# Block sums of the second MLP weights: adding transfers in place of VectorE sums

## The chip, the cores and the metric

The kernel runs on one core of one Trainium2 chip. The metric is the device time of one execution in microseconds. Most executions of a kernel agree within 0.3%. A profile is taken of one further execution by the hardware profiler; its span runs from the first instruction to the last. The engines are TensorE (PE in the profile; its weight loads are the row PEld), VectorE (DVE), ScalarE (ACT), GpSimd (POOL) and SyncE (SP). SP and GpSimd issue the DMAs of this kernel; SP's transfers and GpSimd's run through different DMA queues.

## What is computed

Two decoder layers over 512 tokens of width 1024, in fp32. Each layer has a token mixer (a state-space mixer in layer 0, a gated linear recurrence in layer 1), a normalization, an MLP with 4096 hidden units, another normalization, and a gated input embedding. The change touches the MLP alone:

```python
def sq_relu_mlp(h, w1, w2):
    a = jax.nn.relu(h @ w1)
    return (a * a) @ w2

# in each layer i
h = layer_norm(DEEPNORM_ALPHA * x + mix, ln_g[i, 0], ln_b[i, 0])
h = layer_norm(DEEPNORM_ALPHA * h + sq_relu_mlp(h, mlp_w1[i], mlp_w2[i]), ln_g[i, 1], ln_b[i, 1])
x = h + jax.nn.sigmoid(h @ ple_w_gate[i]) * (p[i] @ ple_w_proj[i])
```

## The kernel before

**Precision.** Every fp32 product is made of three matmuls (`mm3`, lines 119-122): each operand is split into a high and a low part, and high x high, high x low and low x high are added up in PSUM. `split` (lines 109-117) makes the two parts of a weight tile of 128x1024: ScalarE casts it into `whi` (line 113), VectorE subtracts that from the tile and writes `wlo` (line 116). Each of `whi` and `wlo` has six buffers. `unit` (lines 102-107) loads a weight tile through SP into one of three `raw` buffers and splits it.

**The MLP** (`mlp_and_gate`, lines 558-670). The hidden units fall into four groups of 1024. A tile of the first weights, T, is one `project`: 24 matmuls of 128x512 give 128 hidden units for all tokens; ReLU and square follow on ScalarE. Eight tiles make a group. Each group's product with the second weights is a 2x2 block product with seven multiplications in place of eight (the Strassen-Winograd scheme): the hidden activations are cut into blocks a11, a12, a21, a22, the weights into blocks w[0][0], w[0][1], w[1][0], w[1][1], and sums of blocks are multiplied. `half_blocks` (lines 300-320) makes the sums of activations on VectorE and splits each with `put`; it runs twice in a group, once for each half of its tiles. `weight_sums` (lines 322-345) makes the four sums of weight blocks, t1 to t4.

**The weight sums before.** In `weight_sums`, GpSimd issues eight plain loads of 512 KB (line 329) for one group: two halves of each of the four blocks, into eight tiles tagged `r`. VectorE then makes eight sums in place (lines 336, 339, 340 and 344, each for two halves). The tag `r` has eight buffers, all used by one group, so the loads of the next group wait until the splits of this one have read theirs. The same function serves the value projection between the two layers (`values4`, line 675), where the change leaves it as it is.

**The products** (`block_product`, lines 347-395). A product Q is two PSUM banks (c = 0, 1), each of 12 matmuls. `product` splits its weights, multiplies, and lets VectorE empty each bank into the accumulator `acc` (lines 373, 377 and 379); in the last group it also makes row sums for the normalization (line 373). Three sums of products share PSUM: "x" (two banks of the pool `psy`, named `py0` and `py1`) gathers four products one after the other, being read out after each; "y" gathers two and "z" has one (pool `psj`). The products are called p1 (a11), p2 (a12), p3 (s4), p4 (a22), p5 (s1), p6 (s2), p7 (s3), by the activation block that they use.

**The order.** `PERIODS` (line 32) sets how tiles and products alternate: eight T for the first group; then three times two T and seven Q with a T between each two, so that the products of a group run among the tiles of the next; and seven Q without any T for the last group. Inside such a period the products came as p1, p2, p6, p7, p5, p4, p3, and in the last group as p1, p7, p6, p4, p5, p2, p3. Each engine works through its own list in order. A scheduler makes these lists when the kernel is built, from priorities and modelled costs; `high_priority(offset=...)` moves instructions ahead, by `LEAD` = 100, `SOON` = 40 or the group's entry of `SUMS` (line 33). In the MLPs TensorE's order is the scheduler's as well, so that the matmuls of neighbouring products can mix.

**Behind the last group**: the second normalization (`norm`), transposes, and the gate. In the second MLP that is `last_gate` (lines 397-556), which uses four more `r` tiles and already makes its own weight sums with transfers that add onto what is in SBUF (lines 401-408, `accum_op=ALU.add`), issued by GpSimd.

Of the kernel before, what the change touches and what calls it, by code (L numbers as in the profile page):

```python
# [12 lines left out]
ALU = mybir.AluOpType  # L13
PSUM = bass.MemoryType.PSUM

P = 128
# [7 lines left out]
ALPHA = 4.0 ** 0.25  # L24
EPS = 1e-5
LEAD = 100
# [6 lines left out]
SUMS = (60, 300, 300, 300)  # L33
# [11 lines left out]
def trunk(ctx: ExitStack, tc, a):  # L45
    nc = tc.nc
# [21 lines left out]
    def mk(p, shape, tag, dt=F32, **kw):  # L68
        return p.tile(list(shape), dt, tag=tag, name=nm(tag), **kw)

    def f32(t):
        return t.bitcast(F32)
# [16 lines left out]
    def tmp(tag, shape, dt=F32):  # L89
        return mk(phase[0], shape, tag, dt, bufs=phase[2].get(tag, 1))  # L90

    def bank(p, tag):
        return mk(p, [P, T], tag)
# [8 lines left out]
    def unit(src, lead=LEAD, after=None):  # L102
        n = src.shape[1]
        with tc.high_priority(offset=lead):
            raw = mk(raws, [P, 1024], "raw")
            nc.sync.dma_start(raw[:, :n], src)
        return split(raw[:, :n], lead, after)

    def split(f, lead=LEAD, after=None):
        n = f.shape[1]  # L110
        with tc.high_priority(offset=lead):
            hi = mk(whip, [P, 1024], "whi", F32R)
            nc.scalar.copy(hi[:, :n], f)  # L113
            lo = mk(wlop, [P, 1024], "wlo", F32R)
            with behind(after):
                nc.vector.tensor_sub(lo[:, :n], f, f32(hi[:, :n]))  # L116
        return hi, lo

    def mm3(out, sh, sl, mh, ml, start, stop, **kw):
        nc.tensor.matmul(out, sh, mh, start=start, stop=False, **kw)  # L120
        nc.tensor.matmul(out, sh, ml, start=False, stop=False, **kw)  # L121
        return nc.tensor.matmul(out, sl, mh, start=False, stop=stop, **kw)  # L122
# [26 lines left out]
    with tc.high_priority(offset=FIRST):  # L149
        zero = nc.const_aps.tensor(0.0, (P, 1), F32)  # L150
        ps = bank(psm, "pm")
# [76 lines left out]
    def behind(ins):  # L228
        return tc.issue_after(ins.ins) if ins is not None else nullcontext()
# [70 lines left out]
    def half_blocks(blk, z0, z1, p):  # L300

        ks = slice(2 * p, 2 * p + 2)
        a11, a12, a21, a22 = z0[:, :, 256:], z1[:, :, 256:], z0[:, :, :256], z1[:, :, :256]

        def put(name, f):
            hi, lo = blk[name][:, 0, ks, :], blk[name][:, 1, ks, :]
            nc.scalar.copy(hi, f)
            nc.vector.tensor_sub(lo, f, f32(hi))

        put("a11", a11)  # L310
        put("a22", a22)
        nc.vector.tensor_add(a22, a21, a22)
        put("a12", a12)
        nc.vector.tensor_sub(a21, a11, a21)
        nc.vector.tensor_sub(a11, a22, a11)
        nc.vector.tensor_sub(a12, a12, a11)
        put("s2", a11)
        put("s3", a21)
        put("s1", a22)
        put("s4", a12)  # L320

    def weight_sums(w, lead, after=None, queue=nc.gpsimd):

        t = [None] * 4
        for i in (2, 1, 3, 0):
            t[i] = [tmp("r", [P, 1024]) for _ in range(2)]

        def load(i, u, src):
            queue.dma_start(t[i][u], src)  # L329

        with tc.high_priority(offset=lead):
            for u in range(2):
                load(0, u, w[0][1][u])
                load(2, u, w[1][1][u])
                with behind(after):
                    nc.vector.tensor_sub(t[2][u], t[2][u], t[0][u])
                load(1, u, w[0][0][u])
                with behind(after):
                    nc.vector.tensor_sub(t[0][u], t[0][u], t[1][u])
                    nc.vector.tensor_add(t[1][u], t[2][u], t[1][u])  # L340
            for u in range(2):
                load(3, u, w[1][0][u])
                with behind(after):
                    nc.vector.tensor_sub(t[3][u], t[3][u], t[1][u])
        return t

    def block_product(w, blk, lead, first, after=None, turns=None, sums=None, low=None):

        t1, t2, t3, t4 = weight_sums(w, lead, after=low)
        seen = set() if first else {(i, j) for i in range(2) for j in range(2)}
        banks = {}

        def product(x, f, name, start, i, j, turns=None):
            us = [split(v) if f in (t1, t2, t3, t4) else unit(v) for v in f]
            if start:
                banks[name] = [bank(psy, "py%d" % c) if name == "x" else bank(psj, "pj") for c in range(2)]
            t = blk[x]
            for c in range(2):  # L360
                ps = banks[name][c]
                sl = slice(c * P, (c + 1) * P)
                for k in range(4):
                    hi, lo = us[k // 2]
                    ks = slice((k % 2) * 512, (k % 2 + 1) * 512)
                    w_ = hi[:, ks], lo[:, ks]
                    mm3(ps, t[:, 0, k, sl], t[:, 1, k, sl], *w_, start and k == 0, k == 3, skip_group_check=True)
                    if turns and (c, k) in ((0, 3), (1, 1)):
                        next(turns)
                d = acc[:, 2 - 2 * i + c, j * 512 : (j + 1) * 512]  # L370
                with tc.high_priority(offset=SOON if after else 0):
                    if after and f in (w[1][0], t1, t4, w[1][1]):
                        nc.vector.tensor_tensor_reduce(
                            d, ps, d, 1.0, 0.0, ALU.add, ALU.add, sums[:, 2 - 2 * i + c, j : j + 1]
                        )
                    elif (i, j) in seen:
                        nc.vector.tensor_add(d, ps, d)
                    else:
                        nc.vector.scalar_tensor_tensor(d, d, ALPHA, ps, ALU.mult, ALU.add)
            seen.add((i, j))  # L380

        p1 = lambda: product("a11", w[0][0], "x", True, 0, 0)
        p2 = lambda: product("a12", w[1][0], "z", True, 0, 0)
        p6 = lambda: product("s2", t2, "x", False, 1, 0)
        p7 = lambda: product("s3", t3, "y", True, 1, 1)
        p5 = lambda: product("s1", t1, "x", False, 1, 1)
        p4 = lambda: product("a22", t4, "y", False, 1, 0)
        p3 = lambda: product("s4", w[1][1], "x", False, 0, 1, turns)
        for f in (p1, p7, p6, p4, p5, p2, p3) if after else (p1, p2, p6, p7, p5, p4, p3):
            f()  # L390
            if after and f is p5:
                after(0), after(1)
            if after and f is p3:
                after(2), after(3)
            yield
# [162 lines left out]
    def mlp_and_gate(layer, h_s, last):  # L558

        w1, w2 = a[f"w1_{layer}"], a[f"w2_{layer}"]  # L560
        blocks = {}
        low = turned_last[0]
# [32 lines left out]
        for g, period in enumerate(PERIODS):  # L595
            if g < 4:
                tiles = hidden(g)
            if g > 0:
                if g == 4:
                    kept = tmp("blk", [P, 2, 4, 256]) if last else None  # L600
                    h_s, after, turned, sums = norm(2 * layer + 1, kept)
                    p_s = (mk(w4, [P, 2, T], "a", F32R), mk(w4, [P, 2, T], "b", F32R))
                    praw = mk(raws, [P, 1024], "raw")
                    nc.sync.dma_start(praw, a[f"pT_{layer}"].rearrange("p k t -> p (k t)"))
                    praw = praw.rearrange("p (k t) -> p k t", k=2)
                    nc.scalar.copy(p_s[0], praw)
                    nc.vector.tensor_sub(p_s[1], praw, f32(p_s[0]))
                w = [[[w2[8 * g - 8 + 4 * i + 2 * j + u] for u in range(2)] for j in range(2)] for i in range(2)]
                products = block_product(w, blocks.pop(g - 1), SUMS[g - 1], g == 1, *((after, turned(0), sums) if g == 4 else ()), low=low if g == 1 else None)
            for op in period:  # L610
                next(tiles if op == "T" else products)

# [29 lines left out]
        for h in range(2):  # L642
            pu = unit(a[f"wp_{layer}"][h])
            gu = [unit(a[f"wg_{layer}"][4 * h + j]) for j in range(4)]
            for c in range(NCH):
                sl = slice(c * P, (c + 1) * P)
                if h == c == 0:
                    turns = turned(1)
# [6 lines left out]
                turns = turned(c + 2) if h == 0 and c < 2 else None  # L655
# [9 lines left out]
                d = acc[:, c, h * 512 : (h + 1) * 512]  # L665
# [66 lines left out]
    ps = bank(psj, "pj")  # L732
    first = [bank(psy, "py0"), bank(psy, "py1"), bank(psj, "pj"), bank(psj, "pj")]
    for k in range(8):
        if k == 4:
            for i in range(8):
                for c in range(NCH):
# [4 lines left out]
                        start=i == 0,  # L742
# [227 lines left out]
    for j in range(17):  # L970
# [6 lines left out]
        if pend is not None:  # L977
            i = j - 1
# [4 lines left out]
            y = tmp("y", [P, T])  # L983
# [3 lines left out]
            for _, n, done, y in half if i % 2 or i >= 14 else ():  # L987
                done()
                w = snw[:, n : n + 1]
# [13 lines left out]
    g, s, ss = outs.pop(0)  # L1003
# [460 lines left out]
```

## Time and profile before

| | us |
|---|---|
| median of 3 runs | 1411.94 |
| lowest and highest of them | 1411.82, 1413.4 |
| span of the profiled execution | 1409.6 |
| TensorE matmul busy | 1404.3 |
| weight loads busy | 1168.1 |
| VectorE busy | 1069.1 |
| ScalarE busy | 763.6 |
| GpSimd busy | 45.8 |

The span is 2.3 us below the median; that much lies around the first and the last instruction. The granted TensorE clock is 1.000 over the whole span. DMAs moved 181.69 MB, 41.95 MB of them through GpSimd's queue.

How to read the rows that follow. A group's row names line, engine and operation, then output tile and input tiles by their names, the shape, the count, then busy time in us and the mean of one in ns, and after the second bar the idle time of that engine just before, with what ended most of it. A timeline's row begins with the start and the duration in us. A row of waits reads: who waited, for whom, in total, how many times, and the longest. Matmuls overlap on TensorE, so a matmul's duration is longer than the distance between the starts of two.

### The profile page before, as it was taken

Reading aid. Unit: us, or ns where it says so; the run is one execution under the profiler, and the core shown is the slowest. Engines: PE = TensorE matmul, PEld = TensorE weight load, DVE = VectorE, ACT = ScalarE, POOL = GpSimd, SP = SyncE. Lnnn points to the kernel's source line nnn. Section 1 sums busy time; section 2 is a strip of 40 time slices with the busy share of each in tenths; the row PEclk is TensorE's granted clock in tenths of the full one; section 3 lists DMA queues with packets and bytes.
Section 4 is the critical chain, followed back from the end, with each engine's and each line's share of the span. In section 5 each row is a group of like instructions: output and inputs, shape, how many; then the busy total and the mean of one; then the engine's idle time right before and its main releaser. Section 6 shows DMA issues by size and latency. Waiting matters only on the chain.

```text
span 1409.6 us, 20400 instructions
## 1 busy us (share of the span) xinstructions
PE 1404.3 (100%) x8001; PEld 1168.1 (83%) x8001; DVE 1069.1 (76%) x1778; ACT 763.6 (54%) x1156; POOL 45.8 (3%) x92
## 2 busy tenths in 40 slices
PE   9999999999999999999999999999999999999998
PEld 7888888888988888888888888888898888888887
DVE  7989688698977668677986577678785867667795
ACT  7766465573354444545555547655555454544573
POOL 0000000001000000000000000000100000000100
PEclk9999999999999999999999999999999999999999
DMA  8433333234433444345621421222443444444731
GB/s 313 135 117 120 106 120 110 85 100 156 141 113 127 157 131 152 129 142 178 209 90 49 134 91 61 76 87 96 150 135 105 147 137 148 144 137 159 202 106 60
DMA packets 50399, 181.69 MB, mean 129 GB/s; under 512 B 5632, under 2 KB 6400, under 8 KB 50176
## 3 DMA queue, kind: packets, MB, share of 16 engines
q1 hardware_dynamic: 38784, 138.45, 29.6%
q0 software_dynamic: 11520, 41.95, 9.2%
q8 instruction: 63, 1.03, 0.3%
q14 instruction: 32, 0.26, 0.1%
HBM read 177.16 MB, written 2.16 MB: 127 GB/s over the span
## 4 chain that ended last, share of the span: by engine, by line
PE 99%; DMA 0%; DVE 0%; issue 0%; DVEq 0%
PE pj L120 25%; PE pj L121 25%; PE pj L122 25%; PE py L120 5%; PE py L122 5%; PE py L121 5%; PE py L906 1%; PE pt L238 1%; PE py L1175 1%; PE pm L923 1%; PE pm L871 1%; PE py L1301 1%; PE pt L859 0%; PE py L1303 0%; PE py L1240 0%; PE py L832 0%
## 5 line engine op out<-in xcount | busy, mean ns | idle before, releaser
L113 ACT CAST whi<-raw 128x1024 fp32r<-128x1024 f32 x218 | 228.8, 1050 | 333.2 <-PE pj L121 243.6
L120 PE MATMUL pj<-b,whi 128*128 128x512 f32 (+1 forms) x990 | 378.6, 383 | 0.0
L122 PE MATMUL pj<-b,wlo 128*128 128x512 f32 (+1 forms) x990 | 376.8, 381 | 0.0
L121 PE MATMUL pj<-b,whi 128*128 128x512 f32 (+1 forms) x990 | 376.6, 381 | 0.0
L116 DVE TENSOR_TENSOR wlo<-raw,whi 128x1024 fp32r<-128x1024 f32 x218 | 265.4, 1221 | 129.4 <-ACT whi L113 128.2
L121 PEld LDWEIGHTS pj<-b,whi 128*128 128x128 f32 x990 | 186.4, 188 | 34.6 <-issue 0.9
L122 PEld LDWEIGHTS pj<-b,wlo 128*128 128x128 f32 x990 | 186.3, 188 | 34.5
L120 PEld LDWEIGHTS pj<-b,whi 128*128 128x128 f32 x990 | 186.1, 188 | 34.0
L122 PE MATMUL pj<-whi,b 128*128 128x512 f32 x520 | 204.1, 392 | 0.0
L120 PE MATMUL pj<-whi,b 128*128 128x512 f32 x508 | 202.1, 398 | 0.0
L121 PE MATMUL pj<-wlo,b 128*128 128x512 f32 x508 | 199.2, 392 | 0.0
L113 ACT CAST whi<-r 128x1024 fp32r<-128x1024 f32 x76 | 80.0, 1053 | 68.5 <-PE pj L122 39.4
L122 PEld LDWEIGHTS pj<-whi,b 128*128 128x128 f32 x520 | 97.7, 188 | 20.1
L120 PEld LDWEIGHTS pj<-whi,b 128*128 128x128 f32 x508 | 95.5, 188 | 19.1 <-ACT b L1322 0.3
L121 PEld LDWEIGHTS pj<-wlo,b 128*128 128x128 f32 x508 | 95.5, 188 | 18.7 <-issue 0.2
L116 DVE TENSOR_TENSOR wlo<-r,whi 128x1024 fp32r<-128x1024 f32 x76 | 92.5, 1220 | 19.6 <-ACT whi L113 19.1
L122 PE MATMUL py<-whi,b 128*128 128x512 f32 x260 | 101.3, 390 | 0.0
L121 PE MATMUL py<-wlo,b 128*128 128x512 f32 x248 | 96.6, 389 | 0.0
L120 PE MATMUL py<-whi,b 128*128 128x512 f32 x248 | 96.4, 390 | 0.0
L329 POOL DMA_DIRECT2D r<-in_w x64 | 34.0, 532 | 1098.8 <-DVE wlo L116 544.3
L122 PEld LDWEIGHTS py<-whi,b 128*128 128x128 f32 x260 | 48.8, 188 | 10.2
L800 DVE SCALAR_TENSOR_TENSOR cv<-pj,cst,cv 128x509 f32<-128x509 f32 (+2 forms) x66 | 48.9, 746 | 10.6 <-ACT cv L797 9.8
(368 smaller groups left out, 1943.5 us busy)
## 6 DMA issues: line engine op xcount, KB each, us to landing
raw<-in_w SPq DMA_DIRECT2D x112, 512.0 KB, 3.3
r<-in_w POOLq DMA_DIRECT2D x64, 512.0 KB, 3.8
raw<-in_wssd SPq DMA_DIRECT2D x36, 512.0 KB, 3.9
a<-csd SPq DMA_DIRECT2D x16, 512.0 KB, 4.1
raw<-in_wso SPq DMA_DIRECT2D x16, 512.0 KB, 3.3
raw<-in_whq SPq DMA_DIRECT2D x16, 512.0 KB, 3.4
raw<-in_wg SPq DMA_DIRECT2D x15, 512.0 KB, 4.0
raw<-in_whvg SPq DMA_DIRECT2D x14, 512.0 KB, 3.4
```

Source lines behind the costliest of these rows:

```text
L113: nc.scalar.copy(hi[:, :n], f)
L116: nc.vector.tensor_sub(lo[:, :n], f, f32(hi[:, :n]))
L120: nc.tensor.matmul(out, sh, mh, start=start, stop=False, **kw)
L121: nc.tensor.matmul(out, sh, ml, start=False, stop=False, **kw)
L122: return nc.tensor.matmul(out, sl, mh, start=False, stop=stop, **kw)
L238: nc.tensor.transpose(pt[:, j * P : (j + 1) * P], src[:, k * P : (k + 1) * P], ident)
L329: queue.dma_start(t[i][u], src)
L800: nc.vector.scalar_tensor_tensor(cv[:, d:], ps[:, : T - d], convw[:, i, k : k + 1], cv[:, d:], ALU.mult, ALU.add)
L871: nc.tensor.matmul(pst_[:, c * P : (c + 1) * P], btok[:, c, :], xw[:, c].rearrange("p h q -> p (h q)"), start=True, stop=True)
L906: mm = nc.tensor.matmul(yds[0][64 * r : 64 * r + 64, sl], xdt[:, 2 * c + r, :], m[:, r, sl], start=True, stop=True)
L923: mm = nc.tensor.matmul(yo[:, c * P : (c + 1) * P], pv[:, c - 1].rearrange("p h q -> p (h q)"), cm[:, c * P : (c + 1) * P], start=True, st ...
L1175: nc.tensor.matmul(pcs[r][bs, at : at + n], kk[r][:, ts], qs, start=True, stop=True)
```

## The change

The sums of second-weight blocks are made by the DMA engines. A group has two tiles `chain` and two tiles `t1`. At first GpSimd loads w[1][1] into `chain` and adds w[0][1] onto it, and loads w[0][1] into `t1` and adds w[0][0] onto that. `chain` as it then stands is the factor of s3. After it is split, w[0][0] is added onto it, which gives the factor of s2; after that split, w[1][0] is added, which gives the factor of a22. [...] The order of the products becomes p1, p2, p7, p6, p5, p4, p3, and in the last group p1, p7, p6, p5, p4, p2, p3. In `half_blocks`, s3 is put ahead of s2. A group takes four of the eight `r` buffers.

```diff
@@ half_blocks
-        nc.vector.tensor_add(a22, a21, a22)
+        nc.vector.tensor_sub(a22, a22, a21)
         put("a12", a12)
         nc.vector.tensor_sub(a21, a11, a21)
-        nc.vector.tensor_sub(a11, a22, a11)
-        nc.vector.tensor_sub(a12, a12, a11)
+        nc.vector.scalar_tensor_tensor(a11, a22, -1.0, a11, ALU.mult, ALU.subtract)
+        nc.vector.scalar_tensor_tensor(a12, a12, -1.0, a11, ALU.mult, ALU.subtract)
+        put("s3", a21)
         put("s2", a11)
-        put("s3", a21)
@@ block_product
-        t1, t2, t3, t4 = weight_sums(w, lead, after=low)
+        chain, t1 = ([tmp("r", [P, 1024]) for _ in range(2)] for _ in range(2))
+
+        def sums_of(t, *blocks, start=True):
+            for n, b in enumerate(blocks):
+                for u in range(2):
+                    if n == 0 and start:
+                        nc.gpsimd.dma_start(t[u], b[u])
+                    else:
+                        nc.gpsimd.dma_start(t[u], b[u], accum_op=ALU.add)
+
+        with tc.high_priority(offset=lead):
+            sums_of(chain, w[1][1], w[0][1])
+            sums_of(t1, w[0][1], w[0][0])
+        grow = {"s3": w[0][0], "s2": w[1][0]}
@@ product
-            us = [split(v) if f in (t1, t2, t3, t4) else unit(v) for v in f]
+            us = [split(v) if f is chain or f is t1 else unit(v) for v in f]
+            if x in grow:
+                with tc.high_priority(offset=LEAD):
+                    sums_of(chain, grow[x], start=False)
...
-                    if after and f in (w[1][0], t1, t4, w[1][1]):
-                        nc.vector.tensor_tensor_reduce(
-                            d, ps, d, 1.0, 0.0, ALU.add, ALU.add, sums[:, 2 - 2 * i + c, j : j + 1]
-                        )
+                    op = ALU.subtract if j else ALU.add
+                    if after and x in ("a12", "s1", "a22", "s4"):
+                        total = sums[:, 2 - 2 * i + c, j : j + 1]
+                        if j:
+                            nc.vector.scalar_tensor_tensor(d, ps, -1.0, d, ALU.mult, ALU.add, accum_out=total)
+                        else:
+                            nc.vector.tensor_tensor_reduce(d, ps, d, 1.0, 0.0, ALU.add, ALU.add, total)
                     elif (i, j) in seen:
-                        nc.vector.tensor_add(d, ps, d)
+                        nc.vector.tensor_tensor(d, d, ps, op)
                     else:
-                        nc.vector.scalar_tensor_tensor(d, d, ALPHA, ps, ALU.mult, ALU.add)
+                        nc.vector.scalar_tensor_tensor(d, d, ALPHA, ps, ALU.mult, op)
...
-        p6 = lambda: product("s2", t2, "x", False, 1, 0)
-        p7 = lambda: product("s3", t3, "y", True, 1, 1)
+        p6 = lambda: product("s2", chain, "x", False, 1, 0)
+        p7 = lambda: product("s3", chain, "y", True, 1, 1)
         p5 = lambda: product("s1", t1, "x", False, 1, 1)
-        p4 = lambda: product("a22", t4, "y", False, 1, 0)
+        p4 = lambda: product("a22", chain, "y", False, 1, 0)
         p3 = lambda: product("s4", w[1][1], "x", False, 0, 1, turns)
-        for f in (p1, p7, p6, p4, p5, p2, p3) if after else (p1, p2, p6, p7, p5, p4, p3):
+        for f in (p1, p7, p6, p5, p4, p2, p3) if after else (p1, p2, p7, p6, p5, p4, p3):
             f()
-            if after and f is p5:
+            if after and f is p4:
                 after(0), after(1)
```

The normalization of the first two token chunks (`after(0)`, `after(1)`) follows p4, now the fifth product of the last group, where it followed p5. The first group's sums no longer wait behind the last transpose (`low`).

More of the change, by code (lines that the diff above doesn't have):

```diff
@@ L345, in weight_sums, with block_product @@
         return t
-    def block_product(w, blk, lead, first, after=None, turns=None, sums=None, low=None):
-        t1, t2, t3, t4 = weight_sums(w, lead, after=low)
+    def block_product(w, blk, lead, first, after=None, turns=None, sums=None):
+        chain, t1 = ([tmp("r", [P, 1024]) for _ in range(2)] for _ in range(2))
[10 more added lines that the diff above has]
+        grow = {"s3": w[0][0], "s2": w[1][0]}
         seen = set() if first else {(i, j) for i in range(2) for j in range(2)}
@@ L608, in mlp_and_gate @@
                 w = [[[w2[8 * g - 8 + 4 * i + 2 * j + u] for u in range(2)] for j in range(2)] for i in range(2)]
-                products = block_product(w, blocks.pop(g - 1), SUMS[g - 1], g == 1, *((after, turned(0), sums) if g == 4 else ()), low=low if g == 1 else None)
+                products = block_product(w, blocks.pop(g - 1), SUMS[g - 1], g == 1, *((after, turned(0), sums) if g == 4 else ()))
             for op in period:
```

## The prediction

> **What bounds the kernel now.** I read the busy shares first, then the chain of work that ended last, then who waited for whom on TensorE, then busy time by stretches of 100 us.
>
> ```profile
> span 1409.6 us, 20400 instructions
> ...
> PE 1404.3 (100%) x8001; PEld 1168.1 (83%) x8001; DVE 1069.1 (76%) x1778; ACT 763.6 (54%) x1156; POOL 45.8 (3%) x92
> ...
> PE 99%; DMA 0%; DVE 0%; issue 0%; DVEq 0%
> ```
>
> ```profile
> PE pm L153 <- PEq L1452: 0.8, 1, 0.8
> PE py L749 <- DVE b L167: 0.6, 1, 0.6
> ```
>
> The chain is TensorE for 99% of its length, and the second fence is the whole list of waits ahead of matmuls: 0.8 and 0.6 us, both at the start. VectorE, which the change relieves, is busy 76% of the span and holds nobody back for long enough to be listed.
>
> ```profile
> 400.00:500.00 100.00, 100.00 (x443) 82.81 (x442) 67.77 (x80) 51.52 (x67) 4.24 (x8) 1.00 0.40 128
> 500.00:600.00 100.00, 100.00 (x443) 82.81 (x442) 68.77 (x81) 47.19 (x58) 5.29 (x10) 1.00 0.43 141
> ...
> 1100.00:1200.00 100.00, 100.00 (x443) 82.80 (x442) 74.70 (x87) 48.75 (x60) 5.43 (x11) 1.00 0.43 141
> 1200.00:1300.00 100.00, 100.00 (x443) 82.84 (x442) 69.33 (x80) 46.87 (x58) 5.15 (x10) 1.00 0.45 151
> ```
>
> These are windows inside the two MLPs. After the length come, for TensorE matmul, weight load, VectorE, ScalarE and GpSimd, busy time and count; then the granted clock, the DMA share and GB/s. Each window holds the same 443 matmuls at clock 1.00, while VectorE varies from 67.77 to 74.70 us and the DMA share from 0.40 to 0.45. A busy matmul row could hide holes, since matmuls overlap; a count that doesn't move can't. TensorE runs at its own pace.
>
> Here the Trainium skill speaks against my reading: "Perfetto Trace Analysis", section "Identifying the Most-Contended Engine", says that matmul busy share is no good measure of closeness to the limit and that the busy share of weight loads should be used. That share is 83% here, which would leave room. What that could give is priced as a rival below.
>
> **The change, part by part.**
>
> Removed. Each MLP has four groups of hidden units; for each group VectorE made eight sums of 128x1024.
>
> ```profile
> L339 DVE TENSOR_TENSOR r<-r,r 128x1024 f32<-128x1024 f32 x18 | 22.0, 1223 | 16.4 <-DMA r<-in_w 16.2
> L340 DVE TENSOR_TENSOR r<-r,r 128x1024 f32<-128x1024 f32 x18 | 22.0, 1220 | 0.2
> L336 DVE TENSOR_TENSOR r<-r,r 128x1024 f32<-128x1024 f32 x18 | 21.9, 1224 | 30.8 <-DMA r<-in_w 30.8
> L344 DVE TENSOR_TENSOR r<-r,r 128x1024 f32<-128x1024 f32 x18 | 21.9, 1223 | 11.1 <-DMA r<-in_w 10.5 <-DVE wlo L116 0.4
> ```
>
> Of each 18, two are the value projection's, which keeps this code. 4 x 16 = 64 sums of 1.22 us are 78 us of VectorE, and its waits for these loads (up to 58 us) go with them. All of it lies beside TensorE at full pace. It shortens the path by 0.
>
> Replaced on VectorE, at no cost: the half-block edits and the emptying of PSUM keep their number and shapes.
>
> ```profile
> L314 DVE TENSOR_TENSOR a<-a 128x512 f32<-128x512 f32 x16 | 11.0, 690 | 0.3
> L315 DVE TENSOR_TENSOR a<-b,a 128x512 f32<-128x512 f32 x16 | 11.0, 685 | 0.1
> L500 DVE SCALAR_TENSOR_TENSOR blk<-blk 128x512 f32<-128x512 f32 x1 | 0.7, 684 | 0.0
> L379 DVE SCALAR_TENSOR_TENSOR acc<-acc,py 128x512 f32<-128x512 f32 x12 | 8.2, 684 | 2.6 <-PE py L122 2.6
> L377 DVE TENSOR_TENSOR acc<-py,acc 128x512 f32<-128x512 f32 x44 | 30.0, 685 | 5.1 <-PE py L122 5.1
> ...
> L1323 DVE SCALAR_TENSOR_TENSOR b<-pm,cst,b 128x512 fp32r<-128x512 f32 x4 | 3.0, 751 | 2.0 <-ACT b L1322 2.0
> ```
>
> A scaled subtraction (L500) takes 684 ns where the plain one takes 685. The trace has no scaled addition with a running total; scaled ones of this shape take 684 (L379) to 751 ns (L1323), so eight of them cost between 0 and 8 x 0.07 = 0.5 us of VectorE more than now. On the path I take 0: nothing waits for VectorE there.
>
> Added on GpSimd's queue and the DMA engines. A group issued eight plain loads; now it issues four plain loads and eight adding transfers (one addition onto each of the two chain tiles and the two t1 tiles at first, then two growths of the two chain tiles).
>
> ```profile
> L329 POOL DMA_DIRECT2D r<-in_w x64: 527/528/697, 337.4 to 1283.3; - x64
> ...
> L403 POOL DMA_DIRECT2D r<-in_wg x1: 897/897/897, 1308.7 to 1308.7; - x1
> ...
> DMA to landing us min/median/max: 3.6/5.6/8.0
> ```
>
> Issue on GpSimd: 32 x 0.53 + 64 x 0.90 = 74 us in place of 34, on an engine that is 3% busy: 0 on the path. The last line covers the final gate's sums, the only place where adding transfers run now: 5.6 us in the middle, 8.0 at most. I take 5.5 (the median and L403's own value agree) to 8.0 for one growth. The 32 further transfers of 512 KB are 17 MB on engines that are 40 to 45% busy in these windows. Doubling what an adding transfer moves doesn't fill them.
>
> ```profile
> ACT whi L113 <- PE pj L121: 250.9, 85, 5.5
> ...
> ACT whi L113 <- DMA raw<-in_wssd: 8.2, 3, 4.3
> ```
>
> ScalarE's casts wait 250.9 us for a buffer that TensorE still reads, and 8.2 us for the load that they wait for longest: SP's loads come early, and a slower one costs 0.
>
> The Trainium skill's "DMA: Bandwidth & Descriptors", section "Anatomy of one DMA", fits 2.0 us plus bytes over 436 GB/s, about 3.2 us for this size (an estimate from that page). The trace's 5.5 to 8.0 for adding transfers disagrees, and I use the trace.
>
> Moved: the order of products. The sum for s3 must exist first, then grow for s2, then for a22. In the first three groups each product is followed by a tile of the next hidden group, and the splits run far ahead:
>
> ```profile
> 433.56 1.22 DVE L116 TENSOR_TENSOR wlo<-r,whi 128x1024 fp32r<-128x1024 f32 x1
> ...
> 459.09 0.39 PE L120 MATMUL pj<-whi,blk 128*128 128x512 f32 x1
> ```
>
> ```profile
> L113 ACT CAST whi<-r 128x1024 fp32r<-128x1024 f32 x76 | 80.0, 1053 | 68.5 <-PE pj L122 39.4
> ```
>
> The first summed product's split (now s3's) ends at 434.8, so its tile may grow then: landing at 440.3 to 442.8, split again 2.3 us later (1.05 on ScalarE, 1.22 on VectorE), 445.1 at the latest. The next summed product starts at 459.09. That leaves 14 us: 0 on the path.
>
> The last group has no tiles between its products, so there the cover is thin:
>
> ```profile
> 1307.35 1.23 DVE L116 TENSOR_TENSOR wlo<-r,whi 128x1024 fp32r<-128x1024 f32 x1 [3.01 <-ACT whi L113]
> ...
> 1328.24 2.47 DVE L116 TENSOR_TENSOR wlo<-raw,whi 128x1024 fp32r<-128x1024 f32 x2
> 1330.62 0.68 DVE L377 TENSOR_TENSOR acc<-py,acc 128x512 f32<-128x512 f32 x1
> ```
>
> ```profile
> 1312.80 1.05 ACT L113 CAST whi<-r 128x1024 fp32r<-128x1024 f32 x1
> 1313.75 0.61 ACT L307 CAST blk<-a 128x512 fp32r<-128x512 f32 x1
> ```
>
> ```profile
> 1316.50 0.49 PE L122 MATMUL pj<-whi,blk 128*128 128x512 f32 x1
> ...
> 1320.01 0.62 PE L120 MATMUL py<-whi,b 128*128 128x512 f32 x2
> ...
> 1328.19 0.39 PE L120 MATMUL pj<-whi,b 128*128 128x512 f32 x1
> ...
> 1333.63 0.39 PE L120 MATMUL py<-whi,b 128*128 128x512 f32 x1
> ```
>
> From 1328.19 to 1333.63 one product of 24 matmuls runs: 0.227 us each. s3's second tile is split by 1308.6; its growth lands at 1314.1 to 1316.6 and is split by 1316.4 to 1318.9. The s2 product follows the twelve matmuls from 1320.01, at 1322.7. It has at least 3.8 us to spare. The next growth, from 1318.9 at the latest, is split by 1329.2; a22, now behind s1, starts at 1333.63 and has 4.4 us. So 0 for both growths.
>
> One wait is new. s1 now adds onto the PSUM banks that s2 has just filled, and VectorE must read a bank between. From the end of a bank to its reuse lie twelve matmuls, 2.7 us. In this trace s2's second bank ends at 1328.19 and is read until 1331.30, behind two splits (1328.24); it would be needed at 1330.91. That is 0.4 us late in a last group, 0.8 for both MLPs, or 0 if the read goes first. I take the middle, 0.4. Against it stand the two late matmuls of s3 (0.49 in place of 0.39 us, at 1316.50), which the earlier put of s3 may free: 0 to 0.1 each, taken as 0.1 in all.
>
> The sum: 1409.6 + 0.4 - 0.1 = 1409.9 us of span. The median is 2.3 us above the span of the profiled execution, in which start and end stay as they are: **1412.2 us**, no change. About 0.2%, 2.8 us, is what a measurement of this kernel can tell.
>
> **The rivals.**
>
> *ScalarE is held by the growth (slower).* ScalarE works in order. Before, s2's second cast ran at 1312.80, with s3's cast for the other half behind it (1313.75), and TensorE already brushed against that at 1316.50. If the order stays, the cast waits until 1314.1 to 1316.6 and s3's follows 1.05 us later, 1.4 to 3.9 us late; VectorE's part and TensorE wait with it. It decides as soon as the growth lands after 1312.7 with s3 behind it. Twice that is 2.8 to 7.8 us: 1414.7 to 1419.7, middle 1417.2. Against it: s3 is now put ahead of s2. Chance 0.13.
>
> *GpSimd's queue holds a growth (slower).*
>
> ```profile
> L405 POOLq EVENT_SEMAPHORE  x1: 4938/4938/4938, 1309.4 to 1309.4; - x1
> ```
>
> In the second MLP the final gate's transfers use the same queue and wait for one another, 4.9 us here. One such wait ahead of a22's growth takes its 4.4 us and 0.5 more; two cost 5.5. 1412.7 to 1417.7, middle 1415.2. Against it: a group now takes four of the eight tiles, so the gate's transfers can start before the last growths. Chance 0.04.
>
> *VectorE's load slows the matmuls after all (faster).* The windows with 68.77 and 74.70 us of VectorE differ by 5.9 us and by no matmul, so at most by one, 0.23 us. 78 us over some 600 us of MLP are 13 us per window, 2.2 times as much: at most 0.5 us per window, 3.0 in all: 1408.9. That is also where the skill's rule on weight loads would lead; the equal counts speak against it. Chance 0.03.
>
> **How the numbers follow.** No change, 0.80; the first rival 0.13; the second 0.04; the third 0.03. The forecast's own range is 1411.5 to 1413.6 (the run times' spread and 0 to 0.8 us). The two slower rivals lie mostly above 1414.8; the range reaches into the first, to 1416.5, and down to 1410.5. Slower 0.17, within 0.80, faster 0.03.
>
> **What would show it.** Right: TensorE 99% of the chain, 443 matmuls per MLP window, VectorE about 78 us less busy, 96 transfers of r from the second weights. The bank wait would be one longer matmul between s2 and s1 in each last group. The first rival would show as a hole in the s3 product with ScalarE's cast of r waiting for a DMA; the second as a hole ahead of a22. I would be wrong if one growth took more than some 12 us, or if the changed order of instructions opened holes outside the MLPs.

## The result and the profile after

| | before | after |
|---|---|---|
| median of 5 runs each, us | 1412.58 | 1420.15 |
| lowest and highest | 1411.82, 1413.4 | 1416.92, 1422.83 |
| span of the profiled execution | 1409.6 | 1418.4 |

The ratio is 1.0049, with a 95% interval of 1.0035 to 1.0063: slower, by 7.6 us between the medians and by 6.9 us by the ratio (0.0049 x 1412.58). The forecast was 1412.2 and no change; the time lies above its range too. The five runs after lie 5.9 us apart, those before 1.6. From the fastest to the slowest their mean granted TensorE clocks are 1.000, 0.999, 0.998, 0.999 and 0.997, so that part of the loss which the clock makes isn't the same in every execution. The profile below is of the middle one, 1420.15 us.

The page of the kernel after, in the rows that were shown of before:

```profile
span 1418.4 us, 20376 instructions
...
PE 1408.6 (99%) x8001; PEld 1170.2 (83%) x8001; DVE 999.3 (70%) x1714; ACT 763.5 (54%) x1156; POOL 85.3 (6%) x124
...
PE 97%; DMA 2%; DVE 1%; ACT 0%; issue 0%; DVEq 0%; ACTq 0%
```

VectorE lost its 64 instructions (1778 to 1714) and 69.8 us. That is less than 64 x 1.22 = 78, because neighbouring rows on VectorE overlap by some 0.1 us; the single durations added up fall by 79.2 us. TensorE does the same 8001 matmuls, but the chain that ended last now runs through a DMA for 2% and VectorE for 1%. The list of waits ahead of TensorE's matmuls says where:

```profile
PE pt L238 <- DVE b L243: 2.2, 1, 2.2
PE pj L122 <- DVE blk L308: 2.0, 2, 1.0
PE pm L153 <- PEq L1469: 0.8, 1, 0.8
PE py L766 <- DVE b L167: 0.3, 1, 0.3
```

The first two lines are new: one wait of 2.2 us for a transpose's part, and two waits of 1.0 us for an activation block. TensorE's part of the windows inside the MLPs did not change, although VectorE is 10 and 7 us less busy in these two:

```profile
400.00:500.00 100.00, 100.00 (x443) 82.84 (x442) 57.68 (x70) 50.59 (x66) 9.18 (x12) 1.00 0.56 148
500.00:600.00 100.00, 100.00 (x443) 82.84 (x442) 61.69 (x76) 49.83 (x63) 9.14 (x12) 1.00 0.60 163
```

Again 443 matmuls each. To find where the 8.8 us of span come from, I set the start of the k-th matmul after beside that of the k-th before. The distance grows at a few places only, and is flat in between:

| place | distance grows from, to | added, us |
|---|---|---|
| first 57 us of the program | 0 to 1.28 | 1.28 |
| start of the first MLP (before: 374 to 377 us) | 1.28 to 5.24 | 3.96 |
| s3 product of the first MLP's last group (666 us) | 5.24 to 6.79 | 1.55 |
| s3 product of the second MLP's last group (1317 us) | 6.79 to 8.34 | 1.55 |
| behind the last matmuls | 8.3 to 8.8 | 0.5 |

The first row isn't the change's. Up to 382 us TensorE, ScalarE, VectorE and SyncE have the same instructions in the same order before, after and in every kernel below, and GpSimd issues no transfer in the first 57 us; yet in the nine other profiled executions TensorE stands 0.05 us ahead of before (e6) to 1.28 us behind it (after) at 57 us. The kernel e8 below starts 1.05 us late in its profiled execution and still has the median time of the kernel before. The last row isn't explained: from the last matmul to the end take 3.85 to 4.30 us in the ten traces, with no order by kernel that could be seen. What is left, 3.96 + 2 x 1.55 = 7.06 us, is the change's, and its rows are read one by one.

**The start of the first MLP.** Windows of 10 us, first before and then after:

```profile
350.00:360.00 10.00, 10.00 (x49) 8.15 (x48) 8.38 (x13) 1.65 (x4) 0.00 (x0) 1.00 0.89 358
360.00:370.00 10.00, 10.00 (x53) 8.26 (x52) 9.79 (x16) 4.44 (x6) 0.00 (x0) 1.00 0.17 52
370.00:380.00 10.00, 10.00 (x87) 9.87 (x85) 8.51 (x13) 3.59 (x6) 0.00 (x0) 1.00 0.15 54
```

```profile
350.00:360.00 10.00, 10.00 (x48) 8.07 (x47) 8.22 (x13) 0.88 (x2) 2.86 (x4) 1.00 1.02 276
360.00:370.00 10.00, 10.00 (x52) 8.16 (x51) 9.71 (x16) 4.87 (x8) 2.87 (x4) 1.00 1.04 260
370.00:380.00 10.00, 7.75 (x59) 7.45 (x58) 7.45 (x12) 2.75 (x5) 2.30 (x3) 0.95 1.02 298
```

The last two columns are the DMA share and GB/s. Before, the DMA engines had a short crowd at 350 us and were then nearly idle (0.17, 0.15). After, they are full for 30 us (the share comes out slightly above 1). A group now takes four `r` buffers instead of eight, so the sums of the second group start together with those of the first: GpSimd issues 16 transfers of `r` from 338.7 to 381.0 us, where before it issued 8, the last of them by 349.3 us. SP's loads of raw weights sit among them. The stretch from 366 to 380 us, its DMA issues after and then before (KB each, median us from issue to landing):

```profile
r<-in_w POOLq DMA_DIRECT2D x5, 512.0 KB, 8.1
raw<-in_w SPq DMA_DIRECT2D x2, 512.0 KB, 7.1
```

```profile
raw<-in_w SPq DMA_DIRECT2D x2, 512.0 KB, 3.2
```

The same two raw loads take 7.1 us in place of 3.2. ScalarE's timeline, the same load in the trace of before first, and then after:

```profile
370.48 1.05 ACT L113 CAST whi<-raw 128x1024 fp32r<-128x1024 f32 x1 [1.45 <-DMA raw<-in_w]
371.62 0.59 ACT L242 CAST b<-pt 128x512 fp32r<-128x512 f32 x1
```

```profile
369.28 1.06 ACT L113 CAST whi<-raw 128x1024 fp32r<-128x1024 f32 x1 [0.34 <-PE pj L122]
376.04 1.04 ACT L113 CAST whi<-raw 128x1024 fp32r<-128x1024 f32 x1 [5.70 <-DMA raw<-in_w]
376.99 0.58 ACT L242 CAST b<-pt 128x512 fp32r<-128x512 f32 x1
```

The cast of a raw tile waits 5.70 us for its load, where it waited 1.45. ScalarE works in order, and behind that cast stands the copy of a transpose out of PSUM (L242). TensorE waits for that copy's VectorE half: the 2.2 us of the list. Then the clock:

```profile
376.00:378.00 2.00, 0.10 (x1) 0.00 (x0) 0.40 (x1) 1.53 (x2) 0.86 (x1) 1.00 1.04 268
378.00:380.00 2.00, 1.66 (x10) 1.66 (x11) 1.97 (x5) 0.88 (x2) 0.00 (x0) 0.73 1.06 410
380.00:382.00 2.00, 2.00 (x12) 2.00 (x11) 1.58 (x2) 0.00 (x0) 0.88 (x1) 0.50 1.07 219
382.00:384.00 2.00, 2.00 (x19) 2.00 (x18) 0.00 (x0) 0.16 (x1) 0.00 (x0) 0.92 0.85 125
```

TensorE stands still for most of 376 to 378 us, and in the following windows the granted clock is 0.73, 0.50 and 0.92. What is missing to the full clock is 2 x (0.27 + 0.50 + 0.08) = 1.7 us, as much as 3.4 us at half the clock. With the wait, 2.2 + 1.7 = 3.9, which accounts for the 3.96 us of the table. Up to this place all engines but GpSimd have the order of before, so only the transfers can have done it.

**The s3 product of each last group.** ScalarE, then VectorE, then TensorE in the first MLP:

```profile
666.15 0.62 ACT L307 CAST blk<-b 128x512 fp32r<-128x512 f32 x1
668.35 1.05 ACT L113 CAST whi<-r 128x1024 fp32r<-128x1024 f32 x1 [1.59 <-DMA r<-in_w]
669.30 0.61 ACT L307 CAST blk<-a 128x512 fp32r<-128x512 f32 x1
```

```profile
669.44 1.23 DVE L116 TENSOR_TENSOR wlo<-r,whi 128x1024 fp32r<-128x1024 f32 x1 [1.47 <-ACT whi L113]
...
671.18 0.69 DVE L308 TENSOR_TENSOR blk<-a,blk 128x512 fp32r<-128x512 f32 x1
```

```profile
671.92 0.50 PE L122 MATMUL pj<-whi,blk 128*128 128x512 f32 x1 [0.99 <-DVE blk L308]
```

The cast of s2's second weight tile waits 1.59 us for the growth to land; s3's second activation block is cast right behind it. VectorE stands in the same way: the second part of that weight waits for the cast, and the low part of the block comes behind it. TensorE's s3 product waits for that low part. This is the prediction's first rival, at the low end of the 1.4 to 3.9 us that it gave, and it appears again in the second MLP.

### The profile page after: what moved, and what is told of

It is laid out like the page before. It is cut to its first block, busy times and chain, and to the rows that moved or that the text cites. A ratio compares the mean times of both kernels' runs of the same rounds, so it can differ in the third digit from the quotient of the medians.

```text
span 1418.4 us, 20376 instructions
## 1 busy us (share of the span) xinstructions
PE 1408.6 (99%) x8001; PEld 1170.2 (83%) x8001; DVE 999.3 (70%) x1714; ACT 763.5 (54%) x1156; POOL 85.3 (6%) x124
## 4 chain that ended last, share of the span: by engine, by line
PE 97%; DMA 2%; DVE 1%; ACT 0%; issue 0%; DVEq 0%; ACTq 0%
PE pj L120 25%; PE pj L121 24%; PE pj L122 24%; PE py L120 5%; PE py L122 5%; PE py L121 5%; PE py L923 1%; PE pt L238 1%; PE py L1192 1%; PE pm L888 1%; PE pm L940 1%; DMA r<-in_w 1%; DMA raw<-in_w 1%; PE py L1318 1%; PE pt L876 0%; DVE wlo L116 0%
## 5 line engine op out<-in xcount | busy, mean ns | idle before, releaser
L357 POOL DMA_DIRECT2D r<-in_w x64 | 55.7, 871 | 443.9 <-DVE wlo L116 377.5
L355 POOL DMA_DIRECT2D r<-in_w x32 | 20.3, 636 | 624.7 <-DVE acc L260 337.6
```

The costliest lines, as they stand in the source:

```text
L355: nc.gpsimd.dma_start(t[u], b[u])
L357: nc.gpsimd.dma_start(t[u], b[u], accum_op=ALU.add)
```

## The experiments

Two theories stood for the larger loss: that the adding transfers crowd the DMA engines at the start of the first MLP, or that something else in the new order does it. For the smaller ones: the cast that waits for the growth, or the new order of casts and products. The first four kernels were timed beside the kernel before at 1411.85 us (15 runs), the last four at 1412.42 us (31 runs).

**e1_gate.** The first transfers of groups 2, 3 and 4 are issued behind the first growth of the group ahead.

```diff
-        with tc.high_priority(offset=lead):
+        with tc.high_priority(offset=lead), behind(None if first else grown[0]):
             sums_of(chain, w[1][1], w[0][1])
             sums_of(t1, w[0][1], w[0][0])
...
+                if x == "s3":
+                    grown[:] = [ins]
```

> Edit: the first transfers of groups 2 to 4 of each MLP may only be issued on GpSimd's queue after the first growth of the group ahead; everything else is as in the changed kernel. Theory (crowding): the changed kernel frees four r buffers, so the sums of two groups, 16 transfers, are issued at the start of the first MLP and make a raw load of first weights land 7.5 us after its issue; ScalarE's cast waits, the transposes behind it too, and TensorE loses some 4.0 us there. Then this run loses 4.0 us of its time: 1416.1, and the DMA share between 360 and 380 us falls from 1.0 to well below. Rival (the adding transfers themselves, those of one group being enough): the hole stays, 1420. Both expect the s3 holes of the last groups (1.55 us each) unchanged.

Measured: 1424.81 us, ratio 1.0087 (1.0073 to 1.0100). Only GpSimd's order differs from the kernel after. The loss at the start of the first MLP is gone: against before, the distance of the k-th matmul stays at 0.37 to 0.39 us from 358 to 612 us. But the last groups lose far more, 6.1 us in the first MLP and 7.1 in the second. GpSimd and ScalarE there:

```profile
1314.87 0.88 POOL L429 DMA_DIRECT2D r<-in_wg  x1 [3.67 <-DMA r<-r]
1315.41 2.11 POOL L358 DMA_DIRECT2D r<-in_w  x2
```

```profile
1322.84 1.04 ACT L113 CAST whi<-r 128x1024 fp32r<-128x1024 f32 x1 [6.20 <-DMA r<-in_w]
...
1326.18 0.61 ACT L308 CAST blk<-a 128x512 fp32r<-128x512 f32 x1
```

The growth now stands behind the final gate's chain of transfers (L429) and is issued at 1315.41, where the kernel after issued it at 1311.54. The cast of s2's first weight tile waits 6.20 us for it, in place of 0.60 in the kernel after, and TensorE waits 4.3 us for the block that is cast at 1326.18, behind both of s2's tiles. The clock then adds its own: 0.50 from 1326 to 1330 us here, and 0.50 from 670 to 672 us in the first MLP, behind two holes of 0.8 and 1.0 us. In the first MLP 1.5 of the 6.1 us come another way: a sum for the value projection waits on VectorE for its load.

```profile
632.98 1.22 DVE L337 TENSOR_TENSOR r<-r,r 128x1024 f32<-128x1024 f32 x1 [8.02 <-DMA r<-in_whvg]
634.12 0.68 DVE L398 TENSOR_TENSOR acc<-acc,py 128x512 f32<-128x512 f32 x1
```

The load of `in_whvg` landed late among the transfers that the hold had pushed there (the DMA share is 1.04 from 600 to 630 us, where it is 0.47 to 0.68 in the kernel after), and the emptying of PSUM banks (L398) waited behind it in VectorE's order. What follows: the crowding theory holds at the start of the first MLP, and the total was expected wrongly because the held transfers met others later. The loss at s3 grows with the lateness of the growth.

**e2_s3_first.** In the last group both casts of s2's weights are put behind the cast of the s3 block.

```diff
-            us = [split(v) if f is chain or f is t1 else unit(v) for v in f]
+            pin = s3_put[0] if after and x == "s2" else None
+            us = [split(v, cast=pin) if f is chain or f is t1 else unit(v) for v in f]
```

> Edit: in the last group of each MLP the two casts of the grown tiles for s2 stand behind s3's cast on ScalarE; everything else as in the changed kernel. Theory (ScalarE held by the growth): the s3 product's hole of 1.55 us goes in both MLPs, 3.1 us in all: 1417.0; the cast then runs some 1 to 2 us later, and the s2 product has that to spare. Rival (VectorE's half-block work is late by itself, the order of edits is the cause): the holes stay, 1420, or move to the s2 product. Both expect the hole at the start of the first MLP unchanged.

Measured: 1418.22 us, ratio 1.0039 (1.0026 to 1.0052). The start of the first MLP loses as before (3.9 us by the k-th matmul), and no TensorE wait for `blk` is left. In its place stand others: 2.5 us between 677 and 721 us and 1 us at 1031 us, among them waits for VectorE's emptying of a bank and for a normalization, and 0.7 us at 1325 us. TensorE's order isn't that of the kernel after, though: with the pin its list, as the scheduler made it, differs at 113 places, all in the last groups, so what was lost there isn't the casts' alone. That the s3 hole hangs on the order of these casts fits, with that reservation; the remedy gives back much of what it saves.

**e3_both.** Both edits together.

> Both edits, the gate of the groups' first transfers and s3's cast ahead of the grown tiles' casts. If the two places are all that the change costs, 1420.15 - 4.0 - 3.1 = 1413.0, the same as the kernel before (1412.6) within 0.1%, with TensorE 99% of the chain and no hole over 0.4 us in the MLPs. If adding transfers or the new order cost something elsewhere, 1415 or more stays. No theory expects it to be faster than before by more than 0.2%.

Measured: 1420.22 us, ratio 1.0056 (1.0044 to 1.0069), a miss. The start of the first MLP is clean again, but at 634 us a late value-projection sum costs 2.7 us, 1.5 us are lost behind it in the last group, and in the second MLP 5.2 us around the s3 and s2 products. The head of TensorE's list:

```profile
PE py L121 <- DVE acc L403: 3.6, 3, 2.2
PE py L121 <- ACT a L615: 2.5, 1, 2.5
```

The second line is put down to ScalarE, but in the kernel after the same matmul starts before that activation. What held it is VectorE's emptying of a bank, which ended at 636.69 us behind a value-projection sum that had waited 9.24 us for its load; the matmul starts at 636.83. The orders of TensorE are those of e2. A hold on all groups is no remedy, with or without the pin.

**e4_plain.** The first sums' additions are plain loads. The additions are left out; the growths are as in the kernel after.

```diff
-                    if n == 0 and start:
+                    if start:
                         nc.gpsimd.dma_start(t[u], b[u])
```

> Edit: the eight first sums of a group (four tiles) are made by plain loads in place of adding transfers, in the same order with the same waits, so chain and t1 hold one block and not a sum of two (that part of the computation is left out); the growths still add. Theory (an adding transfer takes the DMA engines about twice as long as a plain one, and that makes the crowd last until the raw load): the hole at the start of the first MLP goes, 1416.1. Rival (16 transfers in place of 8 are crowd enough): the raw load still lands late, by more than 5 us, and most of the 4.0 us stays, 1419 to 1420. Both expect the s3 holes unchanged.

Measured: 1416.12 us, ratio 1.0031 (1.0021 to 1.0040); one of its 11 runs took 3669.77 us. The engines' orders are those of the kernel after, and as many transfers of the same size are issued early, but the loss at the start of the first MLP is gone (the distance stays at 0.82 to 0.85 us up to 657 us), and the s3 holes stay. The windows:

```profile
350.00:360.00 10.00, 10.00 (x50) 8.16 (x49) 8.22 (x13) 0.88 (x2) 3.18 (x6) 1.00 1.02 406
360.00:370.00 10.00, 10.00 (x49) 8.10 (x49) 9.74 (x16) 5.21 (x8) 2.66 (x5) 1.00 0.90 342
370.00:380.00 10.00, 10.00 (x86) 9.96 (x85) 8.60 (x12) 2.95 (x6) 0.53 (x1) 1.00 0.45 170
```

At the same share of 1.02 plain loads move 406 GB/s where the mixture with adding ones moves 276, and the crowd is over in time for the raw loads. So it is the adding form that makes the crowd long enough, not the number of transfers.

**e5_hold_one.** The hold for the second group alone.

```diff
-        with tc.high_priority(offset=lead), behind(None if first else grown[0]):
+        with tc.high_priority(offset=lead), behind(hold):
...
+                products = block_product(..., hold=grown[0] if g == 2 else None)
```

> The first transfers of the second group alone are issued behind the first group's first growth; nothing but GpSimd's own order changes, in the middle groups and the last one it is that of the changed kernel. Theory (the adding transfers of two groups crowd the DMA engines at the start of the first MLP and make a raw load late; the last groups lose 1.55 us each because a cast waits for a growth): the 3.95 us at the start go, the two 1.55 us stay, 1420.15 - 3.95 = 1416.2 us. Rival (any hold on GpSimd's queue is given back later, as when all groups were held, 1424.8): 1419 us or more, with a new wait in the last groups.

Measured: 1416.19 us, ratio 1.0027 (1.0017 to 1.0036), as the theory said. The orders of the four other engines are those of the kernel after, instruction for instruction; on GpSimd a few transfers changed places. The window of 366 to 380 us no longer holds any transfer of `r`, the raw loads land after 3.3 us, and TensorE's list keeps the s3 line alone of the two:

```profile
PE pj L122 <- DVE blk L309: 1.9, 2, 1.0
```

**e6_vector_sums.** The new signs, order and banks, with the sums on VectorE from plain loads, as before.

```diff
-            sums_of(chain, w[1][1], w[0][1])
-            sums_of(t1, w[0][1], w[0][0])
+        t1, t2, t3, t4 = plus_sums(w, lead, after=low)
...
+                    nc.vector.tensor_add(t[2][u], t[2][u], t[0][u])
```

> The new signs, the new order of the products and the new banks, but the sums are made by VectorE from plain loads as in the kernel before. Theory (only the transfers cost): 1412 to 1412.8 us, as before, with no hole of TensorE at 372 to 383 us nor in the last groups' s3. Rival (the order of the products, where the s3 product now comes ahead of the s2 product, or the signs cost by themselves): 1414 us or more, with holes at the s3 or s1 products.

Measured: 1412.68 us, ratio 1.0000 (0.9991 to 1.0008). The order of the products and the new signs (differences of activation blocks taken the other way round, products of the right half subtracted) cost nothing that can be told; no wait at s3 or s1 is left, and the one that TensorE's list adds, 0.3 us, lies behind the last product of the first MLP, at 701.91 us. All of the loss comes from the transfers.

**e7_hold_pin.** As e5, and of s2's two casts in the last group only the second, which waits for the landing, is behind the s3 block's.

```diff
-            us = [split(v) if f is chain or f is t1 else unit(v) for v in f]
+            us = [split(v, cast=pin if u else None) if f is chain or f is t1 else unit(v) for u, v in enumerate(f)]
```

> As e5_hold_one, and in the last group the second of the s2 product's two casts (the one that waits for the growth to land) is pinned behind the cast of the s3 block, so the order on ScalarE differs in one pair of instructions per MLP. Theory: both losses go, 1420.15 - 3.95 - 2 x 1.55 = 1413.1 us, and no PE wait for blk at the s3 products. Rival (the cast that is now late makes the s2 product or what comes behind it late, as 0.6 and 1.3 us were seen when both casts were pinned): 1414.5 to 1416.5 us.

Measured: 1414.19 us, ratio 1.0011 (1.0002 to 1.0020). On ScalarE, VectorE and TensorE one or two instructions per MLP changed places. TensorE's waits are down to the two of the program's start:

```profile
PE pm L154 <- PEq L1478: 0.8, 1, 0.8
PE py L775 <- DVE b L168: 0.3, 1, 0.3
```

The profiled execution has a span of 1410.7 us, 1.1 above before's, and is the fastest of the eleven (1412.45 us). The median lies between the theory's 1413.1 and the rival's 1414.5.

**e8_hold_nogrow.** As e5, with the last group's growths left out, so that its s2 and a22 products take s3's weights.

```diff
-            if x in grow:
+            if x in grow and not after:
```

> As e5_hold_one, but the growths of the last group (four adding transfers per MLP) are left out, so its s2 and a22 products take the weights of the s3 product; the order of casts is unchanged. Theory (the holes of the last groups are the wait of a cast for a growth): the holes go, 1416.2 - 3.1 = 1413.1 us. Rival (the holes come from the new order of ScalarE's casts, not from the landing): they stay, 1416.2 us.

Measured: 1412.64 us, ratio 0.9999 (0.9990 to 1.0008). The casts are in the order of e5, and the same stretch of ScalarE reads:

```profile
661.93 0.62 ACT L308 CAST blk<-b 128x512 fp32r<-128x512 f32 x1
662.45 1.05 ACT L113 CAST whi<-r 128x1024 fp32r<-128x1024 f32 x1
663.40 0.61 ACT L308 CAST blk<-a 128x512 fp32r<-128x512 f32 x1
```

No wait stands ahead of the cast of s2's second tile, and the s3 holes are gone. The order of casts is harmless; the landing behind it is what costs.

Put together, by medians: the hold takes 1420.15 to 1416.19 (3.96 us), leaving out the growths of the last group takes that to 1412.64 (3.55 us), and both sum up to 7.5 of the 7.6 us. That the first equals the 3.96 us of the trace is luck: by the ratios, each to the kernel before in its own session, the parts are 3.1 us (1.0049 to 1.0027) and 4.0 us (1.0027 to 0.9999), and the intervals leave the split open by 2 us or so. Together they make up the loss to 0.1 us either way. Beside the s3 holes the profile of e5 loses 0.8 us at about 703 us and 0.5 us behind s3 in the second MLP; e8 and e4 lose 0.8 and 0.7 us at the first of these places too, where TensorE waits 0.4 to 0.5 us for VectorE to empty a bank. Why, the runs don't show. What stays open besides is the 1.5 us of e7's median above e8's: its profiled execution doesn't show them. In it the pinned cast still waits for the landing:

```profile
672.86 1.05 ACT L114 CAST whi<-r 128x1024 fp32r<-128x1024 f32 x1 [1.15 <-DMA r<-in_w]
```

A slower landing in another execution could reach TensorE; that is argued, not shown. None of these kernels beats the kernel before, and none was expected to: TensorE's pace is the same in all.

## Why the prediction was wrong

- **TensorE bounds, and 64 sums off VectorE are worth 0: right.** 443 matmuls per window with VectorE at 57.68 to 61.69 us. With that the third rival (VectorE slows matmuls) falls: e6, with the sums on VectorE, is as fast as e8, without them. The Trainium skill's "Perfetto Trace Analysis", section "Identifying the Most-Contended Engine", judges the room left on TensorE by the busy share of the weight loads, among others. That share is 83% before and after, and no room showed that taking work off VectorE could use.
- **"Doubling what an adding transfer moves doesn't fill them": wrong at one place.** It was read from windows between 400 and 600 us and above 1100, where it held (shares of 0.56 to 0.69 after). The crowd forms at 350 to 380 us. The half of the `r` buffers that came free was used as an argument against the second rival, but not asked what it starts: the second group's transfers at once.
- **"SP's loads come early, and a slower one costs 0": the step that failed most, 4.0 us.** It was read from ScalarE's waits summed over the whole program. In the MLPs the casts do wait for TensorE; at the start of the first MLP a raw load was already the last to come, with 1.45 us of waiting in the trace of before, so whatever a load took longer had to show on ScalarE. The forecast also had no price for the clock that falls after a hole, 1.7 of the 4.0 us in the profiled execution.
- **"So 0 for both growths": wrong, 1.55 us per last group, 3.1 in all.** The slack of 3.8 us was counted to the s2 product on TensorE. What came due first was another instruction behind the waiting cast on ScalarE, and behind that cast's partner on VectorE. The first rival had mechanism, place and price right, and got a chance of 0.13 for a wrong reason: that s3 is put ahead of s2 does not place s3's second block ahead of s2's second weight cast. Two events of 1.4 to 3.9 us were forecast and 1.55 each was found.
- **The size of a growth: right where it counted.** 5.5 to 8.0 us were taken. The growth that makes the cast wait was issued at 662.86 us and the cast began at 668.35, 5.5 us later. The sign that the forecast named, a growth of more than some 12 us, didn't come; all 64 adding transfers of the MLPs, after:

```profile
DMA to landing us min/median/max: 5.1/6.4/11.4
```

- **The new wait at the PSUM bank between s2 and s1 (0.4) and the shorter s3 wait (0.1): neither is there.** TensorE's list after has no wait of that kind, and outside the two s3 holes the distance to before is flat in both last groups.
- **The second rival** (a growth queued behind the gate's transfers) did not occur in the kernel after. e1 shows that it can, at 1315.41 us.
- **"The median is 2.3 us above the span": 0.6 too much, and without effect.** The span of 1409.6 us was set beside the median of other executions. In the runs of before that were listed later, one execution's time is 1.7 to 1.8 us above its own span.

## What to carry to other kernels

Moving work to DMAs is priced at the place where the transfers will run, which is where their buffers come free, and not by a mean share: ask which load of another queue will then be in flight, and what stands in order behind the instruction that waits for it. A slack counted to the consumer on the bounding engine is not the slack of a wait; the wait costs from the moment that the next instruction on its own engine is due. When a hold on a queue is the remedy, hold the one group that collides, since each held transfer meets something later.

## What the runs showed of the hardware

An adding transfer occupies the DMA engines about twice as long as a plain one of the same size. GpSimd's queue, in the page's table of queues, after, with plain first sums (e4), and before:

```profile
q0 software_dynamic: 16128, 58.73, 18.9%
```

```profile
q0 software_dynamic: 16128, 58.73, 15.5%
```

```profile
q0 software_dynamic: 11520, 41.95, 9.2%
```

From the first two: (0.189 x 1418.4 - 0.155 x 1415.0) x 16 = 780 us of one engine's time for 32 additions, 24 us each on top of a plain transfer. A transfer of the kernel before costs 0.092 x 1409.6 x 16 / 80 = 26 us, four of the 80 being additions. So about 50 against 26. It isn't the crowd that makes the difference: between 400 and 600 us, where the mean DMA share is 0.58, the packets of this queue took 29.9% of the 16 engines' time for 8 plain and 16 adding transfers after, and 13.9% for 18 plain ones before. That is 25 us for a plain transfer and, by difference, some 47 for an adding one.

In the profile after, TensorE's clock halved behind one hole of 2.2 us: the granted clock was 1.00 in the window of the hole (376 to 378 us), 0.50 in the one from 380 us, and 1.00 again for the whole of 400 to 500 us. The length of a hole alone doesn't decide it. In e3 a hole of 2.45 us, from 634.38 to 636.83 us, left the clock as it was, and one of 2.17 us, from 1327.93 to 1330.10 us, lowered it:

```profile
634.00:636.00 2.00, 0.38 (x2) 0.00 (x0) 1.14 (x1) 1.78 (x3) 0.00 (x0) 1.00 0.01 4
636.00:638.00 2.00, 1.17 (x5) 1.02 (x6) 2.00 (x4) 1.44 (x2) 0.00 (x0) 1.00 0.00 0
...
1331.00:1333.00 2.00, 2.00 (x7) 1.55 (x6) 2.00 (x3) 0.13 (x1) 0.00 (x0) 0.58 0.83 164
```

So a hole of this size may cost 1.7 us more in one execution and not in another, which would fit the spread of the five runs after; what decides it, these runs don't show. "TensorE: Matmul & The Clock Gate" of the Trainium skill, section "What's actually happening", has the clock halve after at least one idle window of about 3.4 us; here shorter holes sufficed, 2.2 us in the kernel after.
